# A PSUM bank as VectorE's scratch in a hybrid S5 and attention layer: a three-operation recurrence step, rotary norm through PSUM, parameter copies on ScalarE

## The chip, the cores and the metric

The kernel runs on one core of a Trainium2 chip. The metric is device time in microseconds (us) of one execution; the median of several runs is quoted. Engines are written as in the profile: PE (TensorE matmul), PEld (its weight loads), DVE (VectorE), ACT (ScalarE), POOL (GpSimd), SP (SyncE, which issues most DMAs).

## The reference, cut to what matters

One transformer-like layer on 1024 latent tokens with a prefix of 256 context tokens, width 1024, in fp32. A combined projection of the modulated, normed input gives q, k, v, the S5 input u and gates. q and k are RMS-normed per head of 64 and rotated (2-D rotary). The S5 branch is a complex diagonal recurrence in 32 groups of 64 states, in both directions:

```
q = rms_norm(z[..., Q_OFF:K_OFF]...);  q = rope_2d(q, rope)     # k alike
a_bar = exp(lam * dt);  b_bar = ((a_bar - 1) / lam) * b
state[n] = a_bar * state[n-1] + b_bar @ u[n]                    # scan over tokens
y = sum over directions of Re(C state) + D u
```

Then differential attention over latent and context keys, gated merging of both branches, an output projection and a gated MLP with a width-3 convolution.

## The kernel before

All large matmuls are split into high and low fp32r parts and run as three products. Data is tiled by 128 tokens or channels. `phase_a` makes the projections, the S5 branch and the rotary work; `phase_b` is attention, `phase_c` the merging and the MLP. The change touches `phase_a` alone and what it calls. There the order on each engine is written by the tile planner from the data flow; only the opening (the first five u tiles) and phases b and c have an order written out by hand. Each engine executes its list strictly in order, and SP's DMA list likewise.

Order of the stages in `phase_a` (times of the profiled execution):

- u tiles (to about 110 us): ten projections into PSUM tiles `z`, copied out by ACT.
- the K stage (about 110 to 290 us): two weight slabs of ten tiles each. `project` fills a `z` bank with 24 matmuls; `qk_post` squares it on ACT, sums on DVE (L642), makes the reciprocal root in short operations of 128x8 (L643 to L650, DVE and ACT), multiplies by the rotary tables out of PSUM (L654, L658), adds and scales on POOL and ACT (L659, L664, L665), transposes on PE (L669) and splits the result (L672, L673). Between them lie the steps of `s5_params`, a generator: for each of eight quads of groups, complex products on DVE or POOL (`cmul`, L753 to L758), a negation of `ca` (L841), transposes (L846), copies `dup` and `blk` (L854, L857), a negation of `sc` (L858), small matmuls (L864).
- the V stage (to about 420 us), with the S5 state inputs written to `X` (L919 to L923).
- the Q stage (to about 540 us): 16 tiles through `qk_post`, the adaLN matmuls of `ada_part`, and the chunk recurrence `s5_scan`: 158 steps in sequence on DVE, each of four 128x64 operations (L936 to L939) on the real and imaginary state of one chunk.
- the gate projections, `s5_out_quad` (L957 on), `s5_tail`, then attention from about 820 us.

PSUM has eight banks: `ta` and `tb` (pool psT), one `ada` and five `z` (pool psA). A PSUM pool's tiles are handed out in turn; a tile waits for the last reader of the one that held its place.

Of the kernel before, what the change touches and what calls it, by code (L numbers as in the profile page):

```python
# [12 lines left out]
AF = mybir.ActivationFunctionType  # L13
OP = mybir.AluOpType
AX = mybir.AxisListType
PSUM = bass.MemoryType.PSUM
DRAM = bass.MemoryType.DRAM

P = 128
# [8 lines left out]
HD = 64  # L28
G = 32
GC = 16  # L30
# [4 lines left out]
EPS = 1e-6  # L35
# [103 lines left out]
class Kern:  # L139
# [173 lines left out]
    def phase_a(self):  # L313
        nc, cp, I = self.nc, self.cp, self.I
        self.psT, self.psT_st = self.pool("psT", space=PSUM)
        ps, ps_st = self.pool("psA", space=PSUM)
        ca, ca_st = self.pool("ca")
        self.mask = self.t(ca, [P, GC], "mask")
        self.rows = self.t(ca, [P, 384], "rows")
        self.s5c = self.t(ca, [P, 3, G], "s5c")  # L320
        self.A8a = self.t(ca, [P, 2, G], "A8a")
        self.A8b = self.t(ca, [P, 2, G], "A8b")
        hp, hp_st = self.pool("hT")
        hc, hc_st = self.pool("hTc", "right")
        hTh = [self.t(hp, [P, L], f"hTh{k}", 1, F32R) for k in range(KT)]
# [76 lines left out]
        def modulate(part, rb, ks):  # L402
# [5 lines left out]
            for k, h, l, x, r, c in todo:  # L408
                nc.vector.scalar_tensor_tensor(l, x, self.modT[:, k, r:r + 1], r32(h), op0=OP.add, op1=OP.subtract)

        def project(tt, W, pz=None, ks=range(KT)):
            pz = self.t(ps, [P, 512], "z", 5) if pz is None else pz
            A = (hTh, hTl) if tt < NT else (cTh, cTl)
            tok = slice(tt % NT * P, tt % NT * P + P)
            for k in ks:
                wh, wl = W[0][k // 2][:, k % 2], W[1][k // 2][:, k % 2]
                hh, hl = A[0][k][:, tok], A[1][k][:, tok]
                nc.tensor.matmul(pz, hh, wh, start=k == 0, stop=False)  # L418
                nc.tensor.matmul(pz, hh, wl, start=False, stop=False)  # L419
                nc.tensor.matmul(pz, hl, wh, start=False, stop=k == KT - 1)  # L420
            return pz
# [76 lines left out]
        for tt in range(NKT):  # L498
            u = stage(first[tt] if tt < TA else project(tt, W))
            if tt < NT:  # L500
                nc.scalar.dma_start(self.Ud[:, tt], u)
            else:
                nc.scalar.dma_start(self.Ucd[(tt - NT) * P:(tt - NT + 1) * P], u)
            if tt % 2:
                next(params, None)
        zp, zp_st = self.pool("pk")
        self.rope_tables(zp, "K")
        for s in (0, 1):
# [5 lines left out]
        zp_st.close()  # L514
        for _ in params:
            pass
        xp, xp_st = self.pool("s5x")
        states = self.s5_states_in(xp, ps)
        next(states)
        for s in (2, 3):  # L520
            W = self.load_slab(wp, s)
            for tt in range(NKT):
                v = stage(project(tt, W))
# [21 lines left out]
        for s in range(7, 11):  # L545
            W = self.load_slab(wp, s)
            for mm in range(4):
                m = (s - 7) * 4 + mm
                for hf in range(2):
                    tok = slice(hf * 512, hf * 512 + 512)  # L550
                    pz = self.t(ps, [P, 512], "z", 5)
                    for k in range(KT):
                        wh = W[0][k // 2][:, k % 2, mm * P:mm * P + P]
                        wl = W[1][k // 2][:, k % 2, mm * P:mm * P + P]
                        nc.tensor.matmul(pz, wh, hTh[k][:, tok], start=k == 0, stop=False)  # L555
                        nc.tensor.matmul(pz, wh, hTl[k][:, tok], start=False, stop=False)
                        nc.tensor.matmul(pz, wl, hTh[k][:, tok], start=False, stop=k == KT - 1)
                    g = self.t(gp, [P, 512], "stage", 2)
                    nc.scalar.activation(g, pz, AF.Tanh, scale=0.5, bias=self.hbg[:, m:m + 1])
                    nc.scalar.dma_start(self.Gd[m][:, tok], g)  # L560
                    next(adas, None)
                    if hf and nq < QUADS:
                        if nq % 2 == 0:
                            Yq = self.t(yp, [P, NT, P], "Yq", 1)
                        with self.tc.high_priority():
                            self.s5_out_quad(yp, ps, nq, Yq, xp)
                            nq += 1
                            if nq % 2 == 0:
                                self.s5_transpose(yp, ps, Yq, nq // 2 - 1)
                        if nq == QUADS:  # L570
                            for _ in adas:
                                pass
                            ap_st.close()
                            yp_st.close()
                            xp_st.close()
                            tail = self.s5_tail(ps)
                    elif tail:
                        next(tail, None)
# [56 lines left out]
    def qk_post(self, zp, ps, pz, kind, hs, tt):  # L635

        nc = self.nc
        zv = pz.rearrange("p (h d) -> p h d", h=8)
        sq = self.t(zp, [P, 8, HD], "sq", 1)
        nc.scalar.activation(sq, zv, AF.Square)  # L640
        v = self.t(zp, [P, 8], "qv", 2)
        nc.vector.tensor_reduce(v, sq, axis=AX.X, op=OP.add)  # L642
        nc.vector.tensor_scalar(v, v, 1.0 / HD, EPS, op0=OP.mult, op1=OP.add)  # L643
        r = self.t(zp, [P, 8], "qr", 2)
        tm = self.t(zp, [P, 8], "qt", 2)
        nc.scalar.activation(tm, v, AF.Sqrt)
        nc.vector.reciprocal(r, tm)
        nc.vector.tensor_tensor(tm, r, r, op=OP.mult)
        nc.vector.scalar_tensor_tensor(tm, tm, -0.5, v, op0=OP.mult, op1=OP.mult)
        nc.vector.scalar_tensor_tensor(r, tm, 1.5, r, op0=OP.add, op1=OP.mult)  # L650
        t1 = self.t(zp, [P, 8, HD], "t1", 2)
        if tt < NT:
            ct, st = self.tabs[kind]
            nc.vector.tensor_tensor(t1, zv, ct[:, None, tt].to_broadcast([P, 8, HD]), op=OP.mult)  # L654
            t2 = self.t(zp, [P, 8, 2, 32], "t2", 2)
# [10 lines left out]
        pt = self.pst([P, 4, P])  # L666
# [93 lines left out]
    def s5_params(self, ps):  # L760
# [42 lines left out]
            V.tensor_tensor(f[:, i], f[:, i], den, op=OP.mult)  # L803

        for i in range(2):
            V.tensor_copy(self.A8a[:, i], pw[:, 0, 8])
        V.tensor_scalar(self.A8b[:, 0], pw[:, 1, 8], -1.0, None, op0=OP.mult)
        V.tensor_copy(self.A8b[:, 1], pw[:, 1, 8])

        pin = self.t(sp, [P, 2, 8, n], "pin")  # L810
        pout = self.t(sp, [P, 2, 8, n], "pout")
# [5 lines left out]
        for q in range(QUADS):  # L817
# [20 lines left out]

            self.cmul(E, (ba[:, 0], ba[:, 1]), (pb(pin, 0), pb(pin, 1)), (bc(bb, 0), bc(bb, 1)), tq)
            self.cmul(E, (ca[:, 0], ca[:, 1]), (pb(pout, 0), pb(pout, 1)), (bc(sc, 0), bc(sc, 1)), tq)  # L840
            V.tensor_scalar(ca[:, 1], ca[:, 1], -1.0, None, op0=OP.mult)  # L841
            nc.sync.dma_start(self.Wod[q], ca.rearrange("p i g s c -> p i g (s c)"))
            for i in range(2):
                pt = self.t(ps, [P, 4, P], "ada", 1)
                for g in range(4):
                    nc.tensor.transpose(pt[:, g], ba[:, i, g].rearrange("p s c -> p (s c)"), self.ident)  # L846
                wi = self.t(sp, [P, 4, P], "wi", 1)
                nc.scalar.copy(wi, pt)
                nc.sync.dma_start(self.Wid[q][:, i], wi)
# [1 line left out]
            blk = self.t(sp, [P, 2, 2, 4, 2, GC], "blk", 1)  # L851
            nc.gpsimd.memset(blk, 0.0)
            dup = self.t(sp, [P, 2, 4, 2, GC], "dup", 1)
            V.tensor_copy(dup, bb[:, :, :, None].to_broadcast([P, 2, 4, 2, GC]))  # L854
            for d_ in range(2):
                rs = slice(64 * d_, 64 * d_ + 64)
                V.tensor_copy(blk[rs, d_], bb[rs, :, :, None].to_broadcast([64, 2, 4, 2, GC]))  # L857
            V.tensor_scalar(sc[:, 1], sc[:, 1], -1.0, None, op0=OP.mult)  # L858
            pk = self.t(ps, [P, 272], "ada", 1)
            for o, w, x in ((0, blk[:, 0], ca), (P + GC, blk[:, 1], ca), (P, dup, sc)):  # L860
                for i in range(2):
                    for g in range(4):
# [12 lines left out]
    def s5_states_in(self, xp, ps):  # L875
# [7 lines left out]
        for step in range(QUADS + 2):  # L883
# [30 lines left out]
            if q >= 0:  # L914
                for g in range(4):
                    gg = 4 * q + g
                    px = self.pst([P, 2, NCK]) if g % 2 else self.t(ps, [P, 2, NCK], "z", 5)
                    for i in range(2):
                        nc.tensor.matmul(px[:, i], wis[q][:, i, g], uts[q][:, g], start=True, stop=True)  # L919
                    xo = X[:, :, :, gg].rearrange("p n i -> p i n")  # L920
                    nc.scalar.copy(xo[0:64, :, 0:NCC], px[0:64, :, NCH:])
                    nc.scalar.copy(xo[0:64, :, NCC:], px[0:64, :, 0:NCH])
                    nc.vector.tensor_copy(xo[64:128], px[64:128, :, ::-1])  # L923
# [3 lines left out]
    def s5_scan(self, xp, upto):  # L927

        nc, X = self.nc, self.X
        E = nc.vector.tensor_tensor  # L930
        upto = min(upto, NCH + NCC - 1)
        while self.scan_at < upto:
            i = self.scan_at
            t1 = self.t(xp, [P, 2, G], "sc1", 2)
            t2 = self.t(xp, [P, 2, G], "sc2", 2)
            E(t1, X[:, i - 1], self.A8a, op=OP.mult)  # L936
            E(t2, X[:, i - 1, ::-1], self.A8b, op=OP.mult)
            E(X[:, i], X[:, i], t1, op=OP.add)
            E(X[:, i], X[:, i], t2, op=OP.add)  # L939
            self.scan_at += 1  # L940

    def s5_out_quad(self, sp, ps, q, Yq, xp):
# [766 lines left out]
```

## Time and profile before

| | |
|---|---|
| runs, median | 2124.18 us (2121.9, 2124.18, 2127.36) |
| the profiled execution: its time, and the span from first to last instruction | 2117.7 us, 2115.9 us |
| mean granted TensorE clock | 0.978 |
| busy share PE, DVE, ACT, POOL | 95%, 64%, 40%, 43% |

Busy times of one group add up more than the clock, since an operation starts before the one ahead of it has ended; start-to-start distances in the timeline do not. A PE that is busy is not PE at its peak: at the lower granted clock a matmul takes about twice as long and counts as busy all the same.

### The profile page before, as it was taken

What the parts mean: (1) busy time and instruction counts of PE and PEld (TensorE: products, weight loads), DVE (VectorE), ACT (ScalarE), POOL (GpSimd) and SP (SyncE); (2) the same over time, 40 slices, a digit from 0 to 9 for tenths busy, and PEclk for the clock granted to TensorE, in tenths of its full rate; (3) what the DMA queues carried; (4) which work ended last, traced back from release to release, by engine and by line L of the source; (5) the groups of instructions that cost most, each with busy time, mean ns of one, the idle gap of its engine ahead of it and who ended that gap; (6) DMA issues with size and microseconds to landing.
All of it is one profiled execution on the core that took longest, in us unless ns stands there. A gap on an engine that the chain in (4) does not pass through costs nothing.

```text
span 2115.9 us, 29038 instructions
## 1 busy us (share of the span) xinstructions
PE 2016.6 (95%) x10392; PEld 1643.8 (78%) x10392; DVE 1364.6 (64%) x2591; ACT 840.7 (40%) x1509; POOL 915.0 (43%) x1009
## 2 busy tenths in 40 slices
PE   6988999998999999999999989987999999999999
PEld 4766778866678887999999878765888888878887
DVE  6988944799972133888888654468777777752222
ACT  4434424221222312788888611343444443432100
POOL 1466411233311531366666745643544444455321
PEclk9998999999999999999999999987999999999999
DMA  9345575345667326322331135432222222254212
GB/s 325 111 112 140 123 204 182 111 133 163 186 198 232 112 100 225 112 83 78 94 107 53 39 131 177 151 90 70 100 80 79 82 82 79 80 193 129 67 55 93
DMA packets 164624, 262.48 MB, mean 124 GB/s; under 512 B 28672, under 2 KB 92544, under 8 KB 164480
## 3 DMA queue, kind: packets, MB, share of 16 engines
q1 hardware_dynamic: 154400, 242.28, 37.0%
q10 hardware_dynamic: 10080, 18.35, 2.3%
q8 instruction: 82, 1.34, 0.3%
q14 instruction: 62, 0.51, 0.1%
HBM read 188.68 MB, written 71.89 MB: 123 GB/s over the span
## 4 chain that ended last, share of the span: by engine, by line
PE 70%; DVE 21%; DMA 4%; issue 3%; POOL 1%; ACT 1%; SPq 0%; DVEq 0%; ACTq 0%; POOLq 0%
PE ta L1040 7%; PE d L1268 4%; PE d L1269 4%; PE d L1267 4%; PE up L1488 4%; PE up L1489 4%; PE up L1487 4%; PE sc L1240 3%; PE sc L1241 3%; PE z L1487 3%; PE z L1489 3%; PE z L1488 3%; PE tb L1022 3%; DVE X L939 2%; DVE sc L936 2%
## 5 line engine op out<-in xcount | busy, mean ns | idle before, releaser
L1242 DVE TENSOR_REDUCE mx<-sc 128x1 f32<-128x1280 f32 x128 | 190.7, 1491 | 53.3 <-PE sc L1241 52.3
L597 POOL TENSOR_TENSOR wlo<-wraw,whi 128x1024 fp32r<-128x1024 f32 x40 | 97.3, 2449 | 245.8 <-ACT whi L596 243.8
L418 PE MATMUL z<-whi,hTh 128*128 128x512 f32 x448 | 183.1, 413 | 3.6 <-ACT hTh L407 3.6
L419 PE MATMUL z<-wlo,hTh 128*128 128x512 f32 x448 | 181.7, 407 | 0.3 <-POOL wlo L597 0.3
L420 PE MATMUL z<-whi,hTl 128*128 128x512 f32 x448 | 179.9, 403 | 0.0
L995 ACT ACTIVATE e<-sc,mx 128x1280 f32<-128x1280 f32 x128 | 171.9, 1343 | 12.3 <-DVE mx L1242 10.6
L1664 DVE SCALAR_TENSOR_TENSOR x1b<-d,modT,x1b 128x512 f32<-128x512 f32 x80 | 59.8, 750 | 181.3 <-PE d L1269 181.3
L1040 PE MATMUL ta<-V,at 128*128 128x128 f32 x1280 | 168.1, 275 | 0.7 <-ACT at L1029 0.7
L1040 PEld LDWEIGHTS ta<-V,at 128*128 128x128 f32 x1280 | 155.4, 191 | 1.0 <-ACT at L1029 0.9
L1240 PE MATMUL sc<-K,q 128*128 128x512 f32 (+1 forms) x384 | 147.7, 385 | 0.8 <-ACT e L995 0.8
L1480 POOL TENSOR_TENSOR pl<-s,ph 128x512 fp32r<-128x512 f32 x44 | 65.0, 1479 | 182.5 <-ACT ph L1479 182.5
L1268 PE MATMUL d<-g,whi 128*128 128x512 f32 x352 | 139.8, 397 | 3.1 <-DVE g L1636 3.1
L1685 DVE SCALAR_TENSOR_TENSOR y<-up,small,y 128x896 f32<-128x896 f32 (+1 forms) x176 | 123.7, 744 | 29.5 <-ACT y L1680 28.1
L1267 PE MATMUL d<-g,whi 128*128 128x512 f32 x352 | 139.5, 396 | 0.0
L1269 PE MATMUL d<-g,wlo 128*128 128x512 f32 x352 | 139.3, 396 | 0.0
L1241 PE MATMUL sc<-K,q 128*128 128x512 f32 (+1 forms) x384 | 131.9, 358 | 0.0
L1255 POOL TENSOR_TENSOR wlo<-wraw,whi 128x1024 fp32r<-128x1024 f32 (+1 forms) x36 | 74.9, 2087 | 122.5 <-ACT whi L1254 111.6
L418 PEld LDWEIGHTS z<-whi,hTh 128*128 128x128 f32 x448 | 87.1, 194 | 33.1 <-issue 9.8
L1660 POOL TENSOR_TENSOR wlo<-wraw,whi 128x640 fp32r<-128x640 f32 (+2 forms) x40 | 56.3, 1407 | 116.3 <-ACT whi L1659 115.3
L555 PE MATMUL z<-hTh,whi 128*128 128x512 f32 x256 | 102.4, 400 | 0.0
L420 PEld LDWEIGHTS z<-whi,hTl 128*128 128x128 f32 x448 | 87.3, 195 | 19.3 <-issue 1.0
L419 PEld LDWEIGHTS z<-wlo,hTh 128*128 128x128 f32 x448 | 87.5, 195 | 17.4 <-POOL wlo L597 0.7
(490 smaller groups left out, 5509.0 us busy)
## 6 DMA issues: line engine op xcount, KB each, us to landing
wraw<-in_wup_dram SPq DMA_DIRECT2D x46, 512.0 KB
wraw<-in_win_dram SPq DMA_DIRECT2D x44, 512.0 KB
araw<-in_ada_dram SPq DMA_DIRECT2D x32, 512.0 KB
q<-Qd SPq DMA_DIRECT2D x128, 128.0 KB
Kd<-st SPq DMA_DIRECT2D x80, 128.0 KB
K<-Kd SPq DMA_DIRECT2D x16, 640.0 KB
Fd<-y SPq DMA_DIRECT2D x20, 512.0 KB
graw<-Fd SPq DMA_DIRECT2D x20, 512.0 KB
```

Of the source, the lines that this page charges most:

```text
L418: nc.tensor.matmul(pz, hh, wh, start=k == 0, stop=False)
L419: nc.tensor.matmul(pz, hh, wl, start=False, stop=False)
L420: nc.tensor.matmul(pz, hl, wh, start=False, stop=k == KT - 1)
L995: nc.scalar.activation(em, S[i]["sc"][m][:, :LK], AF.Exp, bias=S[i]["mx"][:, m:m + 1], accum_out=S[i]["l1"] if m else S[i]["l0"])
L1040: nc.tensor.matmul(PO[p][:, j * P:j * P + P], AT[p, kt // 2][:, kt % 2, j * P:j * P + P], W[:, kt], start=kt == 0, stop=kt == NKT - 1)
L1240: nc.tensor.matmul(sc[:, a:b], Q[0][:, m, qs], K[m][:, a:b], start=True, stop=False)
L1241: nc.tensor.matmul(sc[:, a:b], Q[1][:, m, qs], K[m][:, a:b], start=False, stop=True)
L1242: nc.vector.tensor_reduce(S["mx"][:, m:m + 1], sc[:, :LK], axis=AX.X, op=OP.max, negate=True)
L1267: mm(o, W[0][:, k], ah[k], start=k == 0, stop=False)
L1268: mm(o, W[0][:, k], al[k], start=False, stop=False)
L1269: mm(o, W[1][:, k], ah[k], start=False, stop=k == n - 1)
L1487: mm(o, W[0][:, k], bh[k], start=k == 0, stop=False)
```

## The change

Three things change.

1. After the u tiles the PSUM pool psA is closed and psA2 opened, with four `z` banks in place of five, one `ada` bank, and one bank `scr` that only DVE uses. It holds the recurrence coefficients `A8p` (copied there once after `s5_params`), two product buffers `scT`, and four small pairs `qkp`.
2. A recurrence step becomes three DVE operations: one of 128x128 that multiplies the state, read twice by broadcast, with all four coefficient rows, and two 128x64 additions (the second with real and imaginary exchanged). In `qk_post` the sum of squares and the reciprocal root lie in `scr`, and the Newton step is rearranged so that each of its DVE operations has one operand there; the count of DVE operations is the same.
3. In `s5_params` the two negations and the copies `dup` and `blk` go from DVE to ACT (five instructions a quad, eight quads).

```diff
@@ phase_a
+        self.psA = ps
-        self.A8a = self.t(ca, [P, 2, G], "A8a")
-        self.A8b = self.t(ca, [P, 2, G], "A8b")
+        self.A8 = self.t(ca, [P, 2, 2, G], "A8")
+        nz = 5
         def project(tt, W, pz=None, ks=range(KT)):
-            pz = self.t(ps, [P, 512], "z", 5) if pz is None else pz
+            pz = self.t(ps, [P, 512], "z", nz) if pz is None else pz
...
+        ps_st.close()
+        ps, ps_st = self.pool("psA2", space=PSUM)
+        self.psA, nz = ps, 4
+        scr = self.t(ps, [P, 512], "scr", 1)
+        self.A8p = scr[:, 0:128].rearrange("p (j i g) -> p j i g", j=2, i=2)
+        self.scT = [scr[:, 128 * j:128 * j + 128].rearrange("p (j i g) -> p j i g", j=2, i=2) for j in (1, 2)]
+        self.qkp = [[scr[:, 384 + 32 * b + 8 * j:392 + 32 * b + 8 * j] for j in range(2)] for b in range(4)]
+        self.qkn = 0
         zp, zp_st = self.pool("pk")
...
         for _ in params:
             pass
+        nc.vector.tensor_copy(self.A8p, self.A8)
@@ qk_post
+        vp, rp = self.qkp[self.qkn % 4]
+        self.qkn += 1
+        nc.vector.tensor_reduce(vp, sq, axis=AX.X, op=OP.add)
         v = self.t(zp, [P, 8], "qv", 2)
-        nc.vector.tensor_reduce(v, sq, axis=AX.X, op=OP.add)
-        nc.vector.tensor_scalar(v, v, 1.0 / HD, EPS, op0=OP.mult, op1=OP.add)
+        nc.vector.tensor_scalar(v, vp, 1.0 / HD, EPS, op0=OP.mult, op1=OP.add)
...
-        nc.vector.reciprocal(r, tm)
-        nc.vector.tensor_tensor(tm, r, r, op=OP.mult)
-        nc.vector.scalar_tensor_tensor(tm, tm, -0.5, v, op0=OP.mult, op1=OP.mult)
-        nc.vector.scalar_tensor_tensor(r, tm, 1.5, r, op0=OP.add, op1=OP.mult)
+        nc.vector.reciprocal(rp, tm)
+        nc.vector.scalar_tensor_tensor(tm, rp, -0.5, v, op0=OP.mult, op1=OP.mult)
+        nc.vector.tensor_tensor(tm, rp, tm, op=OP.mult)
+        nc.vector.scalar_tensor_tensor(r, tm, 1.5, rp, op0=OP.add, op1=OP.mult)
@@ s5_params
-            V.tensor_scalar(ca[:, 1], ca[:, 1], -1.0, None, op0=OP.mult)
+            nc.scalar.activation(ca[:, 1], ca[:, 1], AF.Copy, scale=-1.0)
...
-            V.tensor_copy(dup, bb[:, :, :, None].to_broadcast([P, 2, 4, 2, GC]))
+            nc.scalar.copy(dup, bb[:, :, :, None].to_broadcast([P, 2, 4, 2, GC]))
...
-                V.tensor_copy(blk[rs, d_], bb[rs, :, :, None].to_broadcast([64, 2, 4, 2, GC]))
-            V.tensor_scalar(sc[:, 1], sc[:, 1], -1.0, None, op0=OP.mult)
+                nc.scalar.copy(blk[rs, d_], bb[rs, :, :, None].to_broadcast([64, 2, 4, 2, GC]))
+            nc.scalar.activation(sc[:, 1], sc[:, 1], AF.Copy, scale=-1.0)
@@ s5_scan
-            t1 = self.t(xp, [P, 2, G], "sc1", 2)
-            t2 = self.t(xp, [P, 2, G], "sc2", 2)
-            E(t1, X[:, i - 1], self.A8a, op=OP.mult)
-            E(t2, X[:, i - 1, ::-1], self.A8b, op=OP.mult)
-            E(X[:, i], X[:, i], t1, op=OP.add)
-            E(X[:, i], X[:, i], t2, op=OP.add)
+            t = self.scT[i % 2]
+            E(t, X[:, i - 1, None].to_broadcast([P, 2, 2, G]), self.A8p, op=OP.mult)
+            E(X[:, i], X[:, i], t[:, 0], op=OP.add)
+            E(X[:, i], X[:, i], t[:, 1, ::-1], op=OP.add)
```

## Rows read from the trace of the kernel before

**Rows 1.** Windows by stage: busy us (count) of PE, PEld, DVE, ACT, POOL; granted clock, DMA share, GB/s.
```profile
70.00:290.00 220.00, 197.41 (x1159) 154.63 (x1158) 198.69 (x470) 85.96 (x234) 125.94 (x113) 0.95 0.50 134
...
380.00:612.00 232.00, 217.51 (x932) 154.11 (x932) 221.63 (x787) 49.13 (x86) 78.05 (x51) 0.97 0.52 160
612.00:820.00 208.00, 207.94 (x1021) 168.90 (x1018) 54.05 (x62) 49.00 (x71) 62.91 (x38) 1.00 0.49 160
```
**Rows 2.** Windows of 10 us in the K stage, columns as before.
```profile
150.00:160.00 10.00, 6.02 (x69) 4.39 (x67) 8.21 (x15) 2.42 (x9) 7.24 (x7) 0.99 0.56 151
160.00:170.00 10.00, 8.95 (x31) 6.88 (x32) 7.77 (x15) 4.02 (x13) 8.50 (x9) 0.67 0.28 59
```
**Rows 3.** Waits of PE, 70 to 290 us: total us, times, longest.
```profile
PE ta L669 <- ACT t L664: 10.6, 7, 4.4
```
**Rows 4.** Waits of ACT, 70 to 290 us.
```profile
ACT qt L646 <- DVE qv L643: 45.2, 14, 5.1
```
**Rows 5.** Waits of PE, 380 to 612 us.
```profile
PE ta L669 <- POOL t L665: 5.6, 3, 4.2
...
PE ada L297 <- DMA araw<-in_ada_dram: 4.0, 2, 3.2
```
**Rows 6.** Timeline of DVE: start, duration.
```profile
407.15 0.23 DVE L936 TENSOR_TENSOR sc<-X,A8a 128x64 f32<-128x64 f32 x1
...
407.43 0.22 DVE L938 TENSOR_TENSOR X<-X,sc 128x64 f32<-128x64 f32 x1
407.68 0.23 DVE L939 TENSOR_TENSOR X<-X,sc 128x64 f32<-128x64 f32 x1
407.94 2.33 DVE L936 TENSOR_TENSOR sc<-X,A8a 128x64 f32<-128x64 f32 x1
...
509.31 0.68 DVE L654 TENSOR_TENSOR t<-z,CQ 128x512 f32<-128x512 f32 x1
509.91 0.68 DVE L658 TENSOR_TENSOR t<-z,SQ 128x512 f32<-128x512 f32 x1
```
**Rows 7.** Timeline of POOL at the same place.
```profile
407.75 7.14 POOL L597 TENSOR_TENSOR wlo<-wraw,whi 128x1024 fp32r<-128x1024 f32 x3 [57.45 <-ACT whi L596]
```
**Rows 8.** Single lines of DVE: duration ns min/median/max, first and last start us.
```profile
L936 DVE TENSOR_TENSOR sc<-X,A8a x158: 182/225/2329, 383.5 to 608.0; 128x64 f32<-128x64 f32 x158
L654 DVE TENSOR_TENSOR t<-z,CQ x16: 633/679/690, 427.7 to 549.3; 128x512 f32<-128x512 f32 x16
L1428 DVE TENSOR_TENSOR act<-x,act x8: 678/680/682, 1417.6 to 1436.3; 128x512 fp32r<-128x512 f32 x8
L870 DVE SCALAR_TENSOR_TENSOR kq<-mask,small,ada x8: 216/229/230, 141.7 to 298.5; 128x16 f32<-128x16 f32 x8
L648 DVE TENSOR_TENSOR qt<-qr x36: 153/160/1254, 118.3 to 555.1; 128x8 f32<-128x8 f32 x36
```
**Rows 9.** Groups of DVE by line and shape, 70 to 290 us: busy, mean ns, idle before.
```profile
L648 DVE TENSOR_TENSOR qt<-qr 128x8 f32<-128x8 f32 x20 | 9.8, 491 | 0.3
L857 DVE COPY blk<-bb 64x256 f32<-64x256 f32 x16 | 8.6, 539 | 0.6 <-POOL blk L852 0.5
L643 DVE TENSOR_SCALAR qv<-qv 128x8 f32<-128x8 f32 x20 | 8.3, 417 | 0.1
L650 DVE SCALAR_TENSOR_TENSOR qr<-qt,qr 128x8 f32<-128x8 f32 x20 | 7.2, 360 | 0.3
L649 DVE SCALAR_TENSOR_TENSOR qt<-qt,qv 128x8 f32<-128x8 f32 x20 | 7.0, 351 | 0.3
L841 DVE TENSOR_SCALAR ca<-ca 128x512 f32<-128x512 f32 x8 | 6.4, 800 | 1.2 <-POOL ca L758 1.2
L854 DVE COPY dup<-bb 128x256 f32<-128x256 f32 x8 | 4.6, 575 | 0.3 <-POOL bb L758 0.3
L858 DVE TENSOR_SCALAR sc<-sc 128x64 f32<-128x64 f32 x8 | 3.7, 460 | 0.0
```
**Rows 10.** Groups of ACT by line and shape, 70 to 290 us.
```profile
L848 ACT COPY wi<-ada 128x512 f32<-128x512 f32 x15 | 8.7, 577 | 10.8 <-PE ada L846 6.9 <-issue 4.0
```

More of the change, by code (lines that the diff above doesn't have):

```diff
@@ L550, in phase_a @@
                     tok = slice(hf * 512, hf * 512 + 512)
-                    pz = self.t(ps, [P, 512], "z", 5)
+                    pz = self.t(ps, [P, 512], "z", 4)
                     for k in range(KT):
@@ L805, in s5_params @@
         for i in range(2):
-            V.tensor_copy(self.A8a[:, i], pw[:, 0, 8])
-        V.tensor_scalar(self.A8b[:, 0], pw[:, 1, 8], -1.0, None, op0=OP.mult)
-        V.tensor_copy(self.A8b[:, 1], pw[:, 1, 8])
+            V.tensor_copy(self.A8[:, 0, i], pw[:, 0, 8])
+        V.tensor_copy(self.A8[:, 1, 0], pw[:, 1, 8])
+        V.tensor_scalar(self.A8[:, 1, 1], pw[:, 1, 8], -1.0, None, op0=OP.mult)
         pin = self.t(sp, [P, 2, 8, n], "pin")
@@ L840, in s5_params @@
             self.cmul(E, (ca[:, 0], ca[:, 1]), (pb(pout, 0), pb(pout, 1)), (bc(sc, 0), bc(sc, 1)), tq)
-            V.tensor_scalar(ca[:, 1], ca[:, 1], -1.0, None, op0=OP.mult)
+            nc.scalar.activation(ca[:, 1], ca[:, 1], AF.Copy, scale=-1.0)
             nc.sync.dma_start(self.Wod[q], ca.rearrange("p i g s c -> p i g (s c)"))
             for i in range(2):
-                pt = self.t(ps, [P, 4, P], "ada", 1)
+                pt = self.t(self.psA, [P, 4, P], "ada", 1)
                 for g in range(4):
@@ L853, in s5_params @@
             dup = self.t(sp, [P, 2, 4, 2, GC], "dup", 1)
-            V.tensor_copy(dup, bb[:, :, :, None].to_broadcast([P, 2, 4, 2, GC]))
+            nc.scalar.copy(dup, bb[:, :, :, None].to_broadcast([P, 2, 4, 2, GC]))
             for d_ in range(2):
                 rs = slice(64 * d_, 64 * d_ + 64)
-                V.tensor_copy(blk[rs, d_], bb[rs, :, :, None].to_broadcast([64, 2, 4, 2, GC]))
-            V.tensor_scalar(sc[:, 1], sc[:, 1], -1.0, None, op0=OP.mult)
-            pk = self.t(ps, [P, 272], "ada", 1)
+                nc.scalar.copy(blk[rs, d_], bb[rs, :, :, None].to_broadcast([64, 2, 4, 2, GC]))
+            nc.scalar.activation(sc[:, 1], sc[:, 1], AF.Copy, scale=-1.0)
+            pk = self.t(self.psA, [P, 272], "ada", 1)
             for o, w, x in ((0, blk[:, 0], ca), (P + GC, blk[:, 1], ca), (P, dup, sc)):
@@ L916, in s5_states_in @@
                     gg = 4 * q + g
-                    px = self.pst([P, 2, NCK]) if g % 2 else self.t(ps, [P, 2, NCK], "z", 5)
+                    px = self.pst([P, 2, NCK]) if g % 2 else self.t(ps, [P, 2, NCK], "z", 4)
                     for i in range(2):
```

## The prediction

> **What bounds the kernel now.** The page's share of PE, 95%, says little by itself: the change acts between the u tiles and the end of the recurrence, so I cut the span there and read busy times by window [rows 1]. After the recurrence, from 612 to 820 us, PE is busy for 207.9 of 208 us at the full granted clock. Nothing upstream is hidden there: whatever brings the start of that stretch forward brings the end forward. In the two stretches ahead of it PE has gaps. In the K stage it is busy 197.4 of 220 us, so 22.6 us idle, and the mean granted clock of 0.95 costs about another 220 x 0.05 = 11 us. In the Q stage it is busy 217.5 of 232 us, 14.5 us idle, and 0.97 costs 232 x 0.03 = 7 us. In these same two stretches DVE is busy 198.7 of 220 and 221.6 of 232 us: there DVE, and not PE, is the full engine. [...]
>
> Next, who ends PE's gaps. In the K stage PE waits most for the scaled tile t of `qk_post`, which ACT writes [rows 3]; ACT in its turn stands for 45.2 us before its square root, which wants the DVE operation L643 [rows 4]. In the Q stage PE waits for POOL's scaling, L665, which wants the DVE root; only the 4.0 us for `araw` are a DMA [rows 5]. Both chains run through DVE's list, in which the short rotary operations stand between parameter work or recurrence steps.
>
> Last, why DVE is full. An undisturbed recurrence step goes from 407.15 to 407.94, 0.79 us for four operations [rows 6]. Then L936 takes 2.33 us for 64 elements, and it does so while POOL runs three L597 back to back, 2.4 us each [rows 7]. The single lines show the rule of it [rows 8]: L936 has a median of 225 ns and a maximum of 2329, L648 160 and 1254; their tensor operands are all in SBUF. L654, with one operand in PSUM, has 679 and 690 in the same stretch: it is never held. So two-SBUF operations wait out a POOL operation, and those with one operand in PSUM do not.
>
> **The change part by part, K stage.** Eight quads lose L841, L854, two L857 and L858 on DVE: 6.4 + 4.6 + 8.6 + 3.7 = 23.3 us [rows 9], waits for POOL included. Of the rotary operations, L643, L648, L649 and L650 cost 8.3 + 9.8 + 7.0 + 7.2 = 32.3 us for 80 instructions [rows 9]. Each now has one operand in PSUM. If none is held and each takes the median of 0.160 us, that is 12.8 us, a saving of 19.5. The dearest I can make them is 0.229 us, by L870, a short operation that reads PSUM and two SBUF tensors [rows 8]: 18.3 us, a saving of 14. I take 19.5, since a long operation shows no toll on PSUM (679 ns for L654 against 680 for L1428, all in SBUF). DVE then needs 198.7 - 23.3 - 19.5 = 156 us, and PE's floor of 220 - 22.6 - 11 = 186 becomes the larger.
>
> ACT takes over five instructions a quad. The nearest row is L848, 577 ns for 128x512 [rows 10]; at that price for each, 40 x 0.577 = 23 us, and at half of it, since four of the five have half the elements or fewer, 11.5. I take 16: ACT goes from 86 to about 102 of 220 us. That is not the bound, but ACT is a link of PE's waits, and the moved negation waits for `ca`, which POOL makes in the even quads. What is queued behind it on ACT is `qk_post`'s square, root and scaling, and PE waits for these. The cost is nothing while `ca` is ready when ACT comes to it, as DVE found it (only 1.2 us of waiting in eight, rows of L841); without that cover see the fourth rival.
>
> A filled pipe of PE at full clock is the best case, 34 us. The chain z, ACT, DVE, ACT, DVE, POOL or ACT, PE stays as long in steps; it only gets shorter holds. I take half, 17 us, with 5 and 30 as the ends.
>
> **Q stage.** The recurrence runs from 383.5 to 608.0 us and one step more, 225 us [rows 8]. In it are 16 rotary tiles, each with four long DVE operations spaced 0.60 us (L654 to L658, [rows 6]) and five short ones at 0.16: 38 + 13 = 51 us. That leaves 174 us for 158 steps, 1.10 each against 0.79 undisturbed; the difference, 49 us, is the holding. The new step has three operations, each needing the one before. An addition that needs the operation just before it starts 0.25 us after it, and the next multiplication 0.26 us after that [rows 6]. The first of the three streams 128 elements in place of 64; at 0.60 us for 512 that is at most 0.07 us more. So 0.26 + 0.26 + 0.33 = 0.85 us: undisturbed the new step is slower than the old one, and its whole gain is that nothing holds it: 158 x 0.85 = 134 us, 40 less. From below: if the wide product costs no more than a narrow one, the step is 0.79 less 0.14 (half of 407.15 to 407.43), 0.65 us, and 103 us in all. From above: if each short PSUM operand costs 0.07 us (L870 less L648, 229 - 160) the step is 1.06 us, 167 us in all, and only 7 are saved. I take 0.85, again by the equality of L654 and L1428.
>
> [...]
>
> PE can win in this stage what is not DMA: 14.5 + 7 - 4 = 17.5 us. DVE falls from 222 to some 180 of 232 us, so the holds in the rotary chain shrink, but the steps still stand in DVE's list between the rotary operations. I take half again, 9 us, with 0 and 17 as ends. An earlier end of the recurrence gives nothing by itself: PE has no idle time after it.
>
> **The banks.** `scr` takes a `z` bank. One tile is about 24 matmuls; PE can run ahead by four tiles and no longer five. Where DVE was the bound the run-ahead is used up once, so the cost is at most one tile. From 70 to 290 us PE has 1159 matmul records in 220 us, 0.19 each, so 24 are 4.6 us; from below nothing, if it fills a gap that is there anyway. The pool change makes `scr`'s first writer wait for the last reader of an old bank, at most the same once more. I take 3 us together. The copy of A8p is one short operation, 0.2 us.
>
> **The sum.** 17 + 9 - 3 = 23 us off. The profiled execution had 2117.7 us, 1.8 more than its span; 2117.7 - 23 = 2095. It was 6.5 us faster than the median of the runs shown, so for the median 2124.2 - 23 = 2101.
>
> **The rivals.** First, *PE gets nearly everything back*: the holds were the only cause of the gaps. For it: no other waits of size are listed but `araw`. Against it: six links per tile remain, in strict order. It gives 34 + 17.5 - 5 = 46 at the most, about 40, so 2084.
>
> Second, *a toll on short PSUM operands*, 0.07 us as worked out above: in the K stage 5.6 us of DVE are lost of 42.8, in the Q stage 33 of the 40. The K gain goes to 15, the Q gain to 2, less 3: 14 off, 2110. [...] It makes the gain smaller, not negative.
>
> Third, *the change does not reach the bound*: DVE is relieved and idles, since the order on each list was laid out with the old distances and PE waits at the same places; the lost bank eats what remains. For it: the waits named are small (10.6 and 5.6 us) beside PE's work. Within 3 us of before, 2121.
>
> Fourth, on the other side, *ACT is held at the head of its list in the K stage*: the negation of `ca` or the copies of `bb` come up before POOL or DVE has made them, and `qk_post`'s ACT work stands behind them. For it: ACT's waits for DVE reach 5.1 us at a time [rows 4], and the producer in even quads is the slower POOL. Against it: DVE stood in the same place and waited only 1.2 us in all. With eight quads it eats the 23 us at 2.9 us per quad; at 5.1 it is 41, 18 more than before, 2142.
>
> **How the numbers follow.** Forecast 0.60 (its own range 2090 to 2112), everything back 0.12, the toll 0.06, no reach 0.11, ACT held 0.11. About 0.3%, 6.4 us, is what a measurement of this kernel can tell from no change (the three runs lie 5.5 us apart). Faster takes the first three, 0.78; same 0.11; slower 0.11. A range from 2082 to 2124 holds the forecast, the toll, the third rival and most of the first; it leaves out the fourth and a little on either side.
>
> **What the changed profile would show.** L936's successor and both additions without durations above 0.5 us, and the step at 0.8 to 0.9 us; if at 1.0 or more, the toll. DVE busy from 70 to 290 us near 160 us and PE gaps there at half; if DVE falls and PE's gaps stay, the third rival. ACT waiting in its own list for `ca` or `bb`: the fourth. A wait of PE's first product for DVE or ACT to leave a `z` bank: the lost bank costs more than I took. The stretch after the recurrence must still have PE full; a gap there would mean that something else, a DMA, is late next, and the forecast would be wrong by it.

## The result and the profile after

The changed kernel takes 2184.73 us (2181.08 to 2186.41, 4 runs) against 2123.04 us for the kernel before on the same chip: ratio 1.0286, 95% interval 1.0264 to 1.0308. It is 62 us slower; 2101 was forecast. The profiled execution took 2185.49 us, with a span of 2183.7 us at a mean granted clock of 0.958 (before: 2115.9 at 0.978).

Windows of the changed kernel, columns as in [rows 1]:

```profile
98.00:180.00 82.00, 25.26 (x288) 17.40 (x287) 51.03 (x78) 20.03 (x46) 58.88 (x62) 0.52 0.32 110
414.00:640.00 226.00, 190.87 (x777) 135.81 (x776) 168.74 (x615) 49.16 (x78) 66.53 (x46) 0.89 0.41 126
640.00:880.00 240.00, 240.00 (x1161) 191.09 (x1160) 63.11 (x76) 58.91 (x83) 73.91 (x43) 1.00 0.53 174
```

And of the kernel before, in the first of these stretches:

```profile
98.00:180.00 82.00, 74.23 (x415) 57.84 (x414) 72.81 (x139) 33.88 (x96) 59.98 (x61) 0.96 0.44 113
```

There are two dents. From 98 to 180 us PE works 25 of 82 us, at a clock of 0.52; before, it was 74 us at 0.96. From 180 to 320 us it is full (140.0 of 140 us), and again after the recurrence, as before. During the recurrence, 414 to 640 us, it has 35 us of gaps and a clock of 0.89, where before it had 14.5 and 0.97 [rows 1]. DVE, which was the full engine in both stretches, now has room in both. Two lines of each kernel, the changed one first, show where the time goes (last copy into `X` and first row maximum of the attention; duration min/median/max, first and last start):

```profile
L936 DVE COPY X<-ta x8: 719/726/739, 352.9 to 414.5; 64x320 f32<-64x320 f32 x8
L923 DVE COPY X<-ta x8: 718/728/740, 321.3 to 382.7; 64x320 f32<-64x320 f32 x8
L1253 DVE TENSOR_REDUCE mx<-sc x128: 1472/1492/1494, 882.6 to 1254.5; 128x1 f32<-128x1280 f32 x128
L1242 DVE TENSOR_REDUCE mx<-sc x128: 1470/1492/1493, 822.2 to 1195.0; 128x1 f32<-128x1280 f32 x128
```

The last copy into `X`, the end of the V stage, starts at 414.5 us (before: 382.7): 32 us lost. The attention starts at 882.6 us (before: 822.2): 60 us, so 28 more are lost between. The rest takes what it took, within 8 us.

**The first dent.** PE's waits in the changed kernel, 98 to 180 us (total, times, longest), to be read beside [rows 3]:

```profile
PE ada L859 <- POOL ba L768: 18.2, 1, 18.2
PE ada L877 <- ACT ca L854: 12.9, 5, 3.9
```

PE's timeline behind the last matmul of the u tiles, which starts at 98.01 us:

```profile
116.58 1.11 PE L859 MATMUL ada<-ident,ba 128*128 128x128 f32 x4 [18.17 <-POOL ba L768]
```

And the single line of the square in `qk_post` (duration min/median/max, first and last start):

```profile
L651 ACT ACTIVATE sq<-z x36: 575/597/606, 185.0 to 632.8; 128x512 f32<-128x512 f32 x36
```

After the last u tile PE's next instruction is a transpose of the parameter work, for which it waits 18 us on POOL; then come the products of one quad after another. The first K tile is squared at 185.0 us; before, it was at 108.7. In PE's list all fifteen `ada` tiles of five quads stand ahead of the first K tile; before, five and a half K tiles (24 matmuls each) stood ahead of the third `ada` tile.

**The second dent.** PE's waits from 414 to 640 us, beside [rows 5]:

```profile
PE z L420 <- DVE t L671: 18.2, 7, 4.6
PE ada L297 <- DMA araw<-in_ada_dram: 9.9, 6, 4.0
```

DVE's timeline between two rotary tiles, beside [rows 6]:

```profile
536.36 0.29 DVE L948 TENSOR_TENSOR scr<-X,scr 128x128 f32<-128x128 f32 x1
536.69 0.22 DVE L949 TENSOR_TENSOR X<-X,scr 128x64 f32<-128x64 f32 x1
536.94 0.22 DVE L950 TENSOR_TENSOR X<-X,scr 128x64 f32<-128x64 f32 x1
537.20 0.29 DVE L948 TENSOR_TENSOR scr<-X,scr 128x128 f32<-128x128 f32 x1
...
541.39 0.69 DVE L654 TENSOR_REDUCE scr<-sq 128x8 f32<-128x512 f32 x1
```

PE now waits for the rotary product L671 to free a `z` bank; of its 35 us of gaps another 9.9 are waits for a DMA. DVE does six recurrence steps in one block, 5 us, and only then the next tile's sum of squares; in its list it is six steps between one sum and the next throughout the Q stage (four before the last), and none is left behind the last sum. Six is what the program issues behind each tile: `self.s5_scan(xp, self.scan_at + 6)`. Before, the number varied from 0 to 9, and the steps that could wait did: 50 of the 158 ran after 560 us, behind the rotary work and under a full PE. The step itself takes 0.84 us (536.36 to 537.20), and nothing holds it. The single lines, beside [rows 8]:

```profile
L948 DVE TENSOR_TENSOR scr<-X,scr x158: 286/295/297, 415.3 to 638.4; 128x128 f32<-128x128 f32 x158
L949 DVE TENSOR_TENSOR X<-X,scr x158: 209/220/223, 415.6 to 638.7; 128x64 f32<-128x64 f32 x158
L656 DVE TENSOR_SCALAR qv<-scr x36: 152/158/168, 187.4 to 639.9; 128x8 f32<-128x8 f32 x36
```

Maxima of 2.3 us have become 0.3.

### The profile page after: what moved, and what is told of

It reads as the page before. It is cut to its first block, busy times and chain, and to the rows that moved or that the text cites. A ratio compares the mean times of both kernels' runs of the same rounds, so it can differ in the third digit from the quotient of the medians.

```text
span 2183.7 us, 28927 instructions
## 1 busy us (share of the span) xinstructions
PE 2025.4 (93%) x10392; PEld 1652.0 (76%) x10392; DVE 1293.9 (59%) x2394; ACT 868.2 (40%) x1557; POOL 908.0 (42%) x1009
## 4 chain that ended last, share of the span: by engine, by line
PE 65%; DVE 4%; issue 2%; DMA 2%; POOL 1%; ACT 1%; SPq 0%; DVEq 0%; POOLq 0%; ACTq 0%
PE ta L1051 7%; PE up L1500 3%; PE up L1498 3%; PE up L1499 3%; PE sc L1251 3%; PE sc L1252 3%; PE d L1280 3%; PE d L1279 3%; PE d L1278 3%; PE z L566 3%; PE z L568 3%; PE z L567 3%; PE z L1498 3%; PE z L1499 3%; PE tb L1033 3%; PE z L1500 3%
## 5 line engine op out<-in xcount | busy, mean ns | idle before, releaser
L672 POOL TENSOR_TENSOR t<-t,t 128x512 f32<-128x512 f32 x32 | 42.3, 1322 | 191.6 <-DVE t L671 72.4
```

## The experiments

The theory after the result had two parts. *Fence*: what is issued after the change of pool gets no bank before everything issued to the old pool is done with it; five parameter quads were issued to it, so the K stage waits for them. *Tied order*: accesses to one scratch bank are kept in the order of the program even where they touch different columns; with the norm and the recurrence in one bank the planner can no longer let steps wait. Rivals: the missing fifth `z` bank; PSUM operands as such; ScalarE.

**e1, the fence alone**, on the kernel before, with five `z` banks:

```diff
+        ps_st.close()
+        ps, ps_st = self.pool("psA2", space=PSUM)
+        self.psA = ps
         zp, zp_st = self.pool("pk")
```

> The kernel before with nothing but the close of the PSUM pool after the u tiles and a new pool with the same five z banks and one ada bank. Theory (the pool change is a fence): the first K projection stands behind all parameter work of the five quads issued before it, PE is idle for most of 98 to 180 us, and the kernel is 30 to 50 us slower, 2153 to 2173. Rival (the bank that scr takes is what costs): with five z banks nothing changes, 2120 to 2127.

Measured: 2160.24 us, ratio 1.0189 (1.0173 to 1.0204), 40 us slower. In the window of the first dent PE does in e1 nearly what it does in the changed kernel, at the same clock, though no work was moved to ACT:

```profile
98.00:180.00 82.00, 22.62 (x280) 15.68 (x280) 63.73 (x104) 8.84 (x16) 56.64 (x62) 0.52 0.31 107
```

**e2, the bank alone**: in the program one `z` tile is taken and written at the start of the K stage and read after the gate projections.

```diff
+        hold = self.t(ps, [P, 512], "z", 5)
+        nc.vector.memset(hold[:, 0:8], 0.0)
...
+        hv = self.t(gp, [P, 8], "hold")
+        nc.vector.tensor_copy(hv, hold[:, 0:8])
```

> The kernel before with one of the five z banks withheld from the K stage on (written once, read once at the end of the stage), no pool change. Rival (lost bank): 20 us or more slower. Theory (fence and order): within 6 us of 2123, as in the prediction's 0 to 5 us for the bank.

Measured: 2121.29 us, 1.0008 (0.9998 to 1.0019). No loss can be seen, but the run does not show that the bank was withheld: the read ran at 87.2 us, right behind the write at 87.0 and ahead of the K stage. The trace of the kernel before shows how many banks were wanted. Counted at the first matmul of each tile, that tile included, at most three `z` tiles of the K stage and four of the Q stage had not yet been read to the end; the fifth bank stood free. In e8 and e13 below, with four and with three `z` banks, it is at most three in both stages. So that PE waits for `z` banks in the changed kernel is the form of the second loss, not its cause.

**e3, the change without the pool change**: `scr` is one of the five `z` tiles.

```diff
-        ps_st.close()
-        ps, ps_st = self.pool("psA2", space=PSUM)
-        self.psA, nz = ps, 4
-        scr = self.t(ps, [P, 512], "scr", 1)
+        scr = self.t(ps, [P, 512], "z", 5)
```

> The changed kernel, with scr taken as one of the five z tiles and no pool change: four z banks are left, everything else as changed. Theory (fence costs 31 us up to the end of the V stage, and scr used by both the recurrence and the rotary norm costs another 30 us in the Q stage by tying their order): 2135 to 2155, PE busy from 98 us on, gaps at the z banks in the Q stage still there. Rival (the Q stage lost only because it came late): 2115 or less.

Measured: 2135.52 us, 1.0076 (1.0061 to 1.0091): 2.1 of the 2.9% are gone. Windows of e3 at both dents:

```profile
98.00:180.00 82.00, 71.33 (x456) 54.96 (x454) 64.70 (x131) 38.53 (x106) 61.35 (x61) 0.97 0.50 131
371.00:595.00 224.00, 187.92 (x784) 135.06 (x784) 168.42 (x616) 49.34 (x78) 67.58 (x47) 0.93 0.42 128
```

The first is closed, and the last copy into `X` starts at 370.1 us, 12.6 earlier than in the kernel before. The second is as it was, 36 us of gaps.

**e14, the pool change with no quad ahead of it**: the u loop issues none, the K loop one every two tiles.

```diff
                 nc.scalar.dma_start(self.Ucd[(tt - NT) * P:(tt - NT + 1) * P], u)
-            if tt % 2:
-                next(params, None)
...
-                if tt % 4 == 3:
+                if tt % 2:
                     next(params, None)
```

> The changed kernel with its pool change, but no parameter quad is issued before the change: the u loop issues none, the K loop one every two tiles. Theory (the fence costs only because five quads stand ahead of it): the loss up to the end of the V stage goes, the loss in the Q stage stays, 2130 to 2150. Rival (closing and opening a pool costs by itself, or the parameter work is late in any case): 2165 or more.

Measured: 2139.70 us, 1.0087 (1.0066 to 1.0107), close to e3; the last copy into `X` starts at 370.4 us, as in e3. The pool change is nearly free when nothing slow has been issued to the old pool. By what rule the planner does this stays open.

**e8, as e3, the norm of the Q stage back in SBUF**, so that there `scr` holds the recurrence alone:

```diff
+        if kind == "K":
             vp, rp = self.qkp[self.qkn % 4]
...
+        else:
+            nc.vector.tensor_reduce(v, sq, axis=AX.X, op=OP.add)
+            nc.vector.tensor_scalar(v, v, 1.0 / HD, EPS, op0=OP.mult, op1=OP.add)
...
```

> As the one before, but the rotary norm uses scr only in the K stage; in the Q stage it is in SBUF as in the kernel before, so that in scr only the recurrence is left. Theory (the shared bank ties the order): the Q stage gets its time back and the kernel is faster than before, 2095 to 2118. Rival (four z banks set the Q stage): as the one before, 2135 to 2155.

Measured: 2088.37 us, 0.9856 (0.9841 to 0.9871): 47 us faster than e3, 32 faster than before. That is more than the theory's range allowed.

**e13, as e3, the norm in a bank of its own** in both stages, three `z` banks left:

```diff
+        scr2 = self.t(ps, [P, 512], "z", 5)
-        self.qkp = [[scr[:, 384 + 32 * b + 8 * j:392 + 32 * b + 8 * j] for j in range(2)] for b in range(4)]
+        self.qkp = [[scr2[:, 384 + 32 * b + 8 * j:392 + 32 * b + 8 * j] for j in range(2)] for b in range(4)]
```

> The changed kernel without the pool change, its rotary norm in a scratch bank of its own in both stages, apart from that of the recurrence; three z banks are left. Theory (one bank shared by both ties their order): free again, and as fast as with the norm of the Q stage in SBUF, 2085 to 2098. Rival (the norm's operations on PSUM are themselves what slows the Q stage): about 2135. Rival (z banks): slower than 2100 with gaps at the z banks.

Measured: 2087.01 us, 0.9847 (0.9825 to 0.9870), the lowest of all. It has every operation of e3 and one `z` bank less, and differs only in the bank that the norm uses. Its window during the recurrence:

```profile
371.00:571.00 200.00, 200.00 (x886) 143.33 (x884) 158.02 (x612) 48.88 (x80) 77.39 (x51) 1.00 0.56 177
```

PE has no gap and the full clock, and in DVE's list the number of steps between two sums of squares varies again. That settles the second loss: it is the shared bank, not PSUM and not the number of `z` banks. Each scratch bank here is also one tile, so whether the order is kept by bank or by tile these runs do not tell.

**e12, as e8, the three-operation step in SBUF**: what does the bank buy, and what the smaller count?

```diff
-        nc.vector.tensor_copy(self.A8p, self.A8)
+        self.A8p = self.A8
+        self.scT = [self.t(xp, [P, 2, 2, G], f"sct{j}") for j in range(2)]
```

> The version without the pool change and with the norm of the Q stage in SBUF, but the recurrence's products and coefficients in SBUF too: three operations a step, all operands in SBUF. Theory (what the bank buys is that POOL does not hold the step): operations of 1 to 2.4 us come back, and the kernel is 10 to 25 us slower than that version, 2098 to 2113. Rival (the gain is the smaller count of operations): within 4 us of it, 2084 to 2093.

Measured: 2110.64 us, 0.9958 (0.9941 to 0.9975), 22 us slower than e8. The single line of its product:

```profile
L958 DVE TENSOR_TENSOR sct<-X,A x158: 274/292/2396, 374.0 to 601.4; 128x128 f32<-128x128 f32 x158
```

The median is that of the bank (295), the maximum is again near the 2.4 us that a POOL operation takes in the kernel before [rows 7], and the recurrence runs from 374.0 to 601.4 us, as long as the four operations of before (383.5 to 608.0, [rows 8]). In e8 it runs from 371 to 570 us.

**e11, the three-operation step in a scratch bank as the only change** of the kernel before; **e6, the moves to ScalarE as the only change**; **e10, e8 with the parameter work back on VectorE**:

```diff
+        scr = self.t(ps, [P, 512], "z", 5)
...
+            t = self.scT[i % 2]
+            E(t, X[:, i - 1, None].to_broadcast([P, 2, 2, G]), self.A8p, op=OP.mult)
```
```diff
-            V.tensor_copy(dup, bb[:, :, :, None].to_broadcast([P, 2, 4, 2, GC]))
+            nc.scalar.copy(dup, bb[:, :, :, None].to_broadcast([P, 2, 4, 2, GC]))
```
```diff
-            nc.scalar.copy(dup, bb[:, :, :, None].to_broadcast([P, 2, 4, 2, GC]))
+            V.tensor_copy(dup, bb[:, :, :, None].to_broadcast([P, 2, 4, 2, GC]))
```

(The last two stand for the five instructions of a quad.)

> The kernel before with the three-operation step in a scratch bank (one of the five z banks) as its only change: rotary norm in SBUF, parameter copies on VectorE. Theory (the two gains are separate): the 21 us of the Q stage alone, 2094 to 2104. Rival (the K stage work hides the gain, or the gain of the Q stage needs the earlier start): above 2108.

> The kernel before with nothing but the parameter copies and signs on ScalarE. Theory (VectorE is the bound of the K stage): 4 to 12 us faster, 2108 to 2116. Rival (ScalarE held at the head of its list): 2124 or more.

> The version without the pool change and with the norm of the Q stage in SBUF, but the parameter copies and signs back on VectorE. Theory (VectorE is the bound of the K stage, and its 23 us count): the 12 us gained up to the end of the V stage shrink to about 5, 2092 to 2099. Rival (ScalarE pays back what VectorE saves): no change, 2085 to 2091.

Measured: e11 2097.43 us, 0.9887 (0.9863 to 0.9911); e6 2108.42 us, 0.9947 (0.9931 to 0.9963); e10 2089.66 us, 0.9858 (0.9840 to 0.9876). For e11 and e6 the theory held. For e10 it did not: beside a norm in PSUM the moves bring nothing that can be told (2089.66 against 2088.37 in e8), though alone they bring 11 us. The K stage from 70 to 290 us, in e6, then e10, then e8:

```profile
70.00:290.00 220.00, 201.19 (x1254) 160.68 (x1253) 188.70 (x432) 103.02 (x277) 125.71 (x113) 0.97 0.51 141
```
```profile
70.00:290.00 220.00, 201.00 (x1242) 159.27 (x1241) 189.16 (x472) 87.64 (x235) 125.68 (x113) 0.96 0.51 138
```
```profile
70.00:290.00 220.00, 199.84 (x1250) 158.38 (x1249) 167.16 (x433) 102.10 (x276) 122.08 (x113) 0.98 0.53 143
```

Either half of the relief takes DVE from 198.7 us [rows 1] to 189. Both together take it to 167, and PE is busy no longer for it. Of PE's 20 us of gaps in e8, 15 are waits for ACT's scaling of t, the kind that was the longest before [rows 3]; why they remain stays open.

## Why the prediction was wrong, step by step

**Held two-SBUF operations, and the step at 0.85 us: right.** The step takes 0.84 us and none is held; e12 shows that this, and not the smaller count, is its gain. The maxima show it: 2396 ns for the product in e12, all operands in SBUF, against 297 for L948 and 223 for L949, one operand in PSUM. By what means POOL holds an operation no run shows. The prediction's rule was a little narrow: before, L643 too, with one input and its output in SBUF, had a maximum of 1376 ns; in its place L656, which reads PSUM, has 168.

**A toll on short PSUM operands: did not come, but for some 20 ns on a write.** L656 takes 158 ns with its operand in PSUM, L648 160 in SBUF [rows 8]; L949 takes 220, L936 225. The reciprocal L660, which writes to PSUM, takes 210 ns, and 190 before. The prediction's estimate from above, 0.07 us for each operand, would have made the step 1.06 us; it takes 0.84.

**K stage, 17 us: right in kind, somewhat large.** Without the fence it is 12.6 us (e3). ACT was put at 102 us, and e8 has 102.1; DVE was put at 156 and has 167. That the two savings on DVE both count in time was wrong, as e10 shows. PE's gaps were to be half; in e8 20 us are left of 22.6, which was the prediction's sign for its third rival. The sign misleads, since a fixed window takes in more work when a stage gets faster: in the same 220 us PE has 1250 matmul records in e8 and 1159 before. The 34 us of which half was taken count 11 us of clock as won with the gaps, which was the author's assumption: with 20 us of gaps e8 has a clock of 0.98 there, with 22.6 it was 0.95 before [rows 1].

**Q stage, 9 us: right in kind, too small.** Without the tie it is 21: in e8 the attention starts at 788.7 us, 33.5 earlier than before, of which the K stage gave 12; in e11, with nothing won in the K stage, it starts at 800.7, 21.5 earlier. "Half again" had no row behind it; in e8 and e13 the gaps of this stage are all gone, and from 371 to 571 us the clock is 1.00 in both.

**The banks, 3 us: the step that failed.** The text held that "the pool change makes `scr`'s first writer wait for the last reader of an old bank, at most the same once more", 4.6 us. Not `scr`'s writer waits but the first K tile, and for five quads of parameter work: 40 us alone (e1), and 2.1%, some 45 us, within the change (against e3). One wait between two instructions was priced where a whole stage could not be issued. The part on the lost bank, 0 to 4.6 us, was right, at its lower end: e13 does without two of the five.

**The tie was not in the prediction at all.** It asked where the holds go, and not what order two uses of one bank force. That costs 47 us (e3 against e8; against e13 it is 49). In the prediction's terms it is the second step that failed, the 9 us of the Q stage: "the steps still stand in DVE's list between the rotary operations" took the order of that list as given, and the stages from `X` to the attention lost 28 us in place of gaining. The third rival came nearest, since it had PE wait because of the order of the lists, but it took the order to be the old one. The fourth did not decide: ACT did wait for `ca`, 14.9 us on POOL between 98 and 180 us, but inside the fence, with no K tile ready behind it; alone, the moves to ACT are 11 us faster (e6).

**The sum as it is**: 32 us gained (e8), 47 lost to the tie and 45 to the fence, 60 us slower; 62 were measured. The terms are differences between neighbouring runs, so that they add up is no proof of its own; with the 40 us that the fence costs alone (e1) the sum is 55.

## What to carry to other kernels

In this kernel one operand in PSUM freed VectorE's short operations from GpSimd (a step's product takes at most 297 ns in the bank, and up to 2396 in SBUF, in e12), and it cost them at most some 20 ns each: look for it where a chain of small two-input operations shares its time with GpSimd. But give each independent chain a scratch bank of its own, since here one bank kept all its users in program order (49 us, e3 against e13). Take the bank as a tile of the pool that is open, and where a pool must be changed in the middle of a stream, move slow work that was issued to the old one behind the change.

## What the runs showed that was not expected

Three `z` banks do as well as five: e13 with three takes 2087.01 us, e8 with four 2088.37, and in the kernel before, with five, no more than four are in use at once in the K and Q stages. And the clock adds to a gap: between 98 and 180 us PE was busy for 25 of 82 us and the granted clock was 0.52, and 0.50 from 116 to 180 us; in the kernel before, two products in a row (L418, L419) start 0.43 us apart at a clock of 0.50 (163.34 and 163.77 us) and 0.23 us apart at 1.00 (167.61 and 167.84 us). At the gaps of the second dent the clock was 0.89, and 1.00 in e13, where there are none.
